# Final norm applied by tokens: TensorE turns the blocks of the finished sum, and one scaling by a column of roots per bank writes the output rows

## Chip, cores and metric

One core of a Trainium2 chip runs the whole program in one launch. The metric is device time in microseconds (us). The kernel before takes 1589.42 us, the median of three runs that lie between 1588.81 and 1590.37.

## The reference, cut to what matters

The program is a block of two layers (a gated MLP mixer with differential attention, then windowed attention with a sink; each followed by a SwiGLU) on 512 tokens of 1024 channels, with a context of 256 tokens beside them. What the change touches is the last line, the norm of the finished residual `h` (512 x 1024, float32) and its gain `g`:

```
def rmsnorm(x, g):
    xf = x.astype(jnp.float32)
    y = xf * lax.rsqrt(jnp.mean(xf * xf, axis=-1, keepdims=True) + EPS)
    return (y * g.astype(jnp.float32)).astype(x.dtype)
...
        h = h + g2 * swiglu(modulate(h, norm2_g[l], sh2, sc2), ffn_w_in[l], ffn_w_out[l])
...
    return rmsnorm(h, final_g)
```

## The kernel before, in words

Activations are kept transposed: channels on the 128 partitions, tokens along the free dimension. The residual is eight tiles `xT` of 128 channels x 512 tokens, held two by two, so that k = 0, 1 share a buffer (named 633 in the order of the program), 2 and 3 the next (634), 4 and 5 (635), 6 and 7 (636). Weights and activations are split in a high and a low part, and every product is three matmuls (`mm3`, L102 to L108).

The end of the program is the end of `ffn(1)`. The last product of the SwiGLU is summed in two halves of the tokens, first the tokens 256 to 511 (`off` = 256), then 0 to 255 (`off` = 0). For each half and each of the eight channel tiles m:

- `s2_part` runs the last matmuls on TensorE (PE) into a PSUM bank `pb` (L106 to L108), and `residual` (L774) adds the bank to `xT` on VectorE (DVE).
- `square` (L787) squares the finished piece on ScalarE (ACT). The squares of m = 0 to 4 are added up on GpSimd (POOL, L791) into `sq`; those of m = 5, 6 and 7 stay apart (`rest`).

Then the norm of a half: `rstd_diag` (L145) multiplies `sq` and the three other tiles with a block of ones, so that PE sums over the channels and a column per 128 tokens comes out (L156, L161). DVE takes the column, adds epsilon (L164), and makes the inverse root by a first guess and three Newton steps on 128 x 2 numbers (L135 to L139, ten instructions). Since tokens lie along the free dimension of `xT`, the roots must become rows: DVE writes them on the diagonals of a tile `dg` (L173), and PE multiplies it with ones (`spread`, L183), which gives a bank with the root of each token in all partitions. ACT copies that bank to `rs` for POOL (`final_rows`, L1484).

`final` (L1487) scales the eight tiles by gain and root. DVE does some in one instruction from the bank (L1496: k = 0 and 1 of the first half, k = 0 to 4 of the second), for the others ACT multiplies by the gain as soon as the squares are taken (L1493), and POOL by `rs` afterwards (L1494). After every second k, SyncE (SP) issues the store of 128 x 2 x 256 numbers (256 KB, in pieces of 1 KB, L1500) to `out`, which is 1024 x 512 and is turned on the host. There are eight such stores, four for each half.

The order on every engine is made by a scheduler from the order of the code, the pools' buffers and `issue_after`, which ties an instruction behind another.

Of the kernel before, what the change touches and what calls it, by code (L numbers as in the profile page):

```python
# [6 lines left out]
F32 = mybir.dt.float32  # L7
# [4 lines left out]
ALU = mybir.AluOpType  # L12
AX = mybir.AxisListType.X

P = 128
D = 1024
KT = D // P
TX = 512
# [8 lines left out]
class Builder:  # L27
# [69 lines left out]
    def dense(self, out, W, A, after=None, first=0):  # L97
        for k in range(len(W)):
            with self.tc.issue_after(after.ins) if after and k >= first else ExitStack():
                self.mm3(out, W[k], A[k], k == 0, k == len(W) - 1)  # L100

    def mm3(self, out, s, m, start, stop):  # L102

# [41 lines left out]
    def rstd_diag(self, accs, inv, bank=None, eps=None, at=None, more=()):  # L145

        nc = self.nc
        nb = sum(T for _, T in accs) // P
        ms = self.small(nb)
        o = 0  # L150
        for acc, T in accs:
            ps = (bank or self.bank)()
            n = T // P
            for j in range(n):
                c = slice(j * P, (j + 1) * P)
                self.last_sum = nc.tensor.matmul(ps[:, c], acc[:, c], self.ones, start=j == 0, stop=not more,  # L156
                                                 skip_group_check=True)
            for t in more:
                for j in range(n):
                    c = slice(j * P, (j + 1) * P)  # L160
                    nc.tensor.matmul(ps[:, c], t[:, c], self.ones, start=False, stop=t is more[-1], skip_group_check=True)  # L161
            col = ps[:, 0:T].rearrange("p (j f) -> p j f", f=P)[:, :, 0]
            if eps is None:
                nc.vector.tensor_scalar(ms[:, o:o + n], col, inv, EPS, ALU.mult, ALU.add)  # L164
            else:
                nc.vector.scalar_tensor_tensor(ms[:, o:o + n], col, inv, eps[:, o:o + n], ALU.mult, ALU.add)
            o += n
        r = self.rsqrt_small(ms, nb)
        dgs, o = [], 0
        for acc, T in accs:  # L170
            dg = at if at is not None else self.tmp()
            for j in range(T // P):
                self.last_diag = nc.vector.tensor_scalar(dg[:, j * P:(j + 1) * P], self.ident, r[:, o + j:o + j + 1], None,  # L173
                                                         ALU.mult)
            dgs.append(dg[:, :T])
            o += T // P
        return dgs
# [680 lines left out]
    def ffn(self, l):  # L858
# [190 lines left out]
        def s2_part(fs, m, W, off, n, chain=False):  # L1049
            ps = self.bank()[:, :n]  # L1050
            A = [(hi[:, off:off + n], lo[:, off:off + n]) for hi, lo in [hid[f] for f in fs]]
            if not chain:
                self.dense(ps, W, A)
                self.residual(l, 5, m, off, n, ps)
                return
            for k in range(len(W)):
                run("PE", self.mm3, ps, W[k], A[k], k == 0, k == len(W) - 1)
            run("DVE", self.residual, l, 5, m, off, n, ps)
# [418 lines left out]
        project(1, catB, lambda m: self.bank())  # L1477
        self.sq = sq, rest[1]

    def final_rows(self, sq, more, off, n):  # L1480
        dg = self.dg[:, off:off + n]
        r = self.rstd_rows(sq[:, off:off + n], n, 1.0 / D, self.single, dg, more, self.bank if off else self.fill)
        rs = self.p0.tile([P, 512], F32, name=self.uid("rs"), tag="tq"[off > 0], bufs=2)[:, :n]
        self.nc.scalar.copy(rs, r)  # L1484
        return r, rs

    def final(self, rows, off, n):  # L1487
        nc = self.nc
        r, rs = rows
        for k in range(KT):  # L1490
            g, h = self.gains[:, 4 * KT + k:4 * KT + k + 1], self.hx[k][:, off:off + n]
            if k >= (2, 5)[off == 0]:
                nc.scalar.mul(h, h, g)  # L1493
                nc.gpsimd.tensor_tensor(h, h, rs, ALU.mult)  # L1494
            else:
                nc.vector.scalar_tensor_tensor(h, h, g, r, ALU.mult, ALU.mult)  # L1496
            nh = self.nh
            if k % nh == nh - 1:
                out = self.a["out"][(k - nh + 1) * P:(k + 1) * P, off:off + n].rearrange("(k p) t -> p k t", p=P)
                nc.sync.dma_start(out, self.hxs[k // nh][:, :, off:off + n])  # L1500


def prep(inp):
# [15 lines left out]
    gains = np.concatenate([A["norm1_g"], A["norm2_g"], A["final_g"][None]], 0)  # L1519
    r["gains"] = c(gains.reshape(5 * KT, P).T)  # L1520
    ew = A["even_w_in"][0]
    r["qk"] = c(ew[:, 1024:2048].reshape(KT, P, 2, 2, 2 * P).transpose(3, 0, 1, 2, 4).reshape(2, KT, P, 512))
    r["v0"] = c(ew[:, 2048:2560])

# [49 lines left out]
```

## Time and profile before

| what | value |
|---|---|
| median of three runs | 1589.42 us |
| the profiled execution's own time | 1588.33 us |
| its span, first to last instruction | 1586.3 us |
| busy, PE / DVE / ACT / POOL | 96% / 68% / 46% / 52% |
| granted TensorE clock, mean | 0.988 |
| HBM written | 2.10 MB |
| end of the last residual product on PE | about 1570.2 us |
| last of the eight stores issued | 1582.63 us |

Times in the profile count from the start of the span. The profiled execution took 1588.33 us, of which 2.0 us lie around the span. PE is busy until 1570.2 us; what follows is the norm of the second half and the stores, 16 us in which PE works little.

### The profile page before, as it was taken

What the parts mean: (1) busy time and instruction counts of PE and PEld (TensorE: products, weight loads), DVE (VectorE), ACT (ScalarE), POOL (GpSimd) and SP (SyncE); (2) the same over time, 40 slices, a digit from 0 to 9 for tenths busy, and PEclk for the clock granted to TensorE, in tenths of its full rate; (3) what the DMA queues carried; (4) which work ended last, traced back from release to release, by engine and by line L of the source; (5) the groups of instructions that cost most, each with busy time, mean ns of one, the idle gap of its engine ahead of it and who ended that gap; (6) DMA issues with size and microseconds to landing.
All of it is one profiled execution on the core that took longest, in us unless ns stands there. A gap on an engine that the chain in (4) does not pass through costs nothing.

```text
span 1586.3 us, 24984 instructions
## 1 busy us (share of the span) xinstructions
PE 1518.7 (96%) x9547; PEld 1352.2 (85%) x9547; DVE 1084.7 (68%) x1958; ACT 723.3 (46%) x1472; POOL 830.7 (52%) x565
## 2 busy tenths in 40 slices
PE   6999988999999999999999989999999999999996
PEld 4776877889989999999999978777869989999996
DVE  4720788765688788888785585765667976666656
ACT  2412676553552333333333244565655644444443
POOL 0463211061256776677676415531304398888883
PEclk9999999999999999999999999999999999999998
DMA  8845100033223333454451012110225132323301
GB/s 328 308 145 188 40 8 1 3 131 133 67 80 113 114 120 106 140 166 147 164 165 57 27 52 80 61 34 14 68 80 206 54 120 88 113 92 109 94 14 54
DMA packets 54295, 162.00 MB, mean 102 GB/s; under 512 B 6176, under 2 KB 10656, under 8 KB 46496
## 3 DMA queue, kind: packets, MB, share of 16 engines
q1 hardware_dynamic: 47120, 135.11, 25.5%
q10 hardware_dynamic: 7056, 25.30, 4.9%
q8 instruction: 75, 1.23, 0.3%
q14 instruction: 44, 0.36, 0.1%
HBM read 158.29 MB, written 2.10 MB: 101 GB/s over the span
## 4 chain that ended last, share of the span: by engine, by line
PE 83%; DVE 10%; ACT 3%; issue 2%; DMA 1%; POOL 0%; POOLq 0%; SPq 0%; DVEq 0%; ACTq 0%
PE pw L106 11%; PE pw L107 11%; PE pw L108 11%; PE pb L107 8%; PE pb L106 8%; PE pb L108 8%; PE pf L106 4%; PE pf L107 4%; PE pf L108 4%; PE pb L1427 2%; PE pb L1416 2%; PE pf L359 2%; PE pw L1379 1%; PE pw L1387 1%; PE pw L542 1%
## 5 line engine op out<-in xcount | busy, mean ns | idle before, releaser
L84 POOL TENSOR_TENSOR w<-raw,w 128x512 fp32r<-128x512 f32 (+1 forms) x84 | 127.5, 1525 | 242.9 <-ACT w L81 220.5
L107 PE MATMUL pw<-ax,w 128*128 128x384 f32 (+2 forms) x732 | 233.9, 320 | 3.7 <-DVE ax L201 2.3
L106 PE MATMUL pw<-ax,w 128*128 128x384 f32 (+2 forms) x732 | 232.9, 322 | 4.1 <-DVE q L879 1.9
L108 PE MATMUL pw<-ax,w 128*128 128x384 f32 (+2 forms) x732 | 233.1, 320 | 0.1
L774 DVE SCALAR_TENSOR_TENSOR xT<-pb,mod,xT 128x512 f32<-128x512 f32 (+3 forms) x208 | 145.7, 707 | 125.8 <-PE pb L108 125.5
L879 POOL TENSOR_TENSOR w<-raw,w 128x512 fp32r<-128x512 f32 x110 | 169.4, 1555 | 19.7 <-ACT w L879 19.5
L879 POOL TENSOR_TENSOR w<-t,w 128x512 fp32r<-128x512 f32 x99 | 148.6, 1504 | 55.6 <-ACT w L879 55.6
L106 PE MATMUL pb<-hh,w 128*128 128x512 f32 x480 | 171.0, 356 | 2.3 <-DVE xT L774 2.3
L108 PE MATMUL pb<-hh,w 128*128 128x512 f32 x480 | 171.5, 357 | 0.3 <-DVE w L879 0.3
L107 PE MATMUL pb<-hh,w 128*128 128x512 f32 x480 | 171.1, 356 | 0.0
L107 PE MATMUL pw<-T,w 128*128 128x384 f32 (+1 forms) x508 | 156.9, 310 | 1.2 <-DVE T L123 1.2
L106 PE MATMUL pw<-T,w 128*128 128x384 f32 (+1 forms) x508 | 156.3, 310 | 1.1 <-DVE hs L879 1.1
L108 PE MATMUL pw<-T,w 128*128 128x384 f32 (+1 forms) x508 | 157.0, 310 | 0.0
L106 PEld LDWEIGHTS pw<-ax,w 128*128 128x128 f32 x732 | 138.5, 190 | 12.5 <-DVE q L879 2.6
L107 PEld LDWEIGHTS pw<-ax,w 128*128 128x128 f32 x732 | 139.0, 190 | 11.2 <-DVE ax L201 3.6
L106 PE MATMUL pf<-ax,w 128*128 128x256 f32 (+2 forms) x420 | 139.9, 333 | 7.9 <-DVE qf L252 5.0
L108 PEld LDWEIGHTS pw<-ax,w 128*128 128x128 f32 x732 | 139.2, 190 | 3.1 <-DVE w L948 0.4
L107 PE MATMUL pf<-ax,w 128*128 128x256 f32 (+2 forms) x420 | 138.8, 330 | 0.0
L108 PE MATMUL pf<-ax,w 128*128 128x256 f32 (+2 forms) x420 | 138.7, 330 | 0.0
L879 POOL TENSOR_TENSOR hh<-hs,hh 128x768 fp32r<-128x768 f32 (+1 forms) x42 | 80.7, 1922 | 90.0 <-ACT hh L879 67.6
L879 POOL TENSOR_TENSOR w<-rawo,w 128x512 fp32r<-128x512 f32 x59 | 103.5, 1754 | 30.1 <-ACT w L879 30.1
L228 DVE SCALAR_TENSOR_TENSOR junk<-ar,cb 128x1024 bf16<-128x1024 f32 x64 | 105.6, 1651 | 0.0
(378 smaller groups left out, 3936.8 us busy)
## 6 DMA issues: line engine op xcount, KB each, us to landing
raw<-ffn_in SPq DMA_DIRECT2D x44, 1024.0 KB, 5.1
ar<-ada SPq DMA_DIRECT2D x24, 1024.0 KB, 6.9
ar<-ada ACTq DMA_DIRECT2D x48, 512.0 KB, 3.5
rawo<-ffn_out SPq DMA_DIRECT2D x88, 256.0 KB, 3.0
raw<-odd_out SPq DMA_DIRECT2D x32, 256.0 KB, 2.7
raw<-qk SPq DMA_DIRECT2D x16, 256.0 KB, 7.9
raw<-uv SPq DMA_DIRECT2D x16, 256.0 KB, 2.7
raw<-even_out SPq DMA_DIRECT2D x8, 512.0 KB, 3.5
```

The lines of the kernel that those rows point to most:

```text
L84: eng.tensor_tensor(lo, raw, hi.bitcast(F32), ALU.subtract)
L106: mm(out, s[0], m[0], start=start, stop=False, **kw)
L107: mm(out, s[0], m[1], start=False, stop=False, **kw)
L108: return mm(out, s[1], m[0], start=False, stop=stop, **kw)
L228: return self.nc.vector.scalar_tensor_tensor(junk, t, 1.0, self.cb[who], ALU.mult, ALU.mult, accum_out=self.acc[who][:, col:col + 1])
L359: nc.tensor.matmul(ps[32 * q:32 * q + 32, :w], cst[:, k, :], t[:, w * q:w * q + w], start=k == 0, stop=k == KT - 1, skip_group_check=True)
L542: nc.tensor.matmul(ps[:, :TX], Q[c][:, qs], K[c][p][:, :TX], start=p == 0, stop=p == 1)
L774: ins = self.nc.vector.scalar_tensor_tensor(h, ps[:, r], self.modcol(l, j, m, who), h, ALU.mult, ALU.add)
L879: tail[key] = fn(*args, **kw)
L1379: nc.tensor.matmul(ps[:, st:en], Q, K[g][p][:, b0 * P:b1 * P], start=p == 0, stop=p == 1, skip_group_check=True)
L1416: last = nc.tensor.transpose(pt[:, x * P:(x + 1) * P], es[2 * (x % 2) + x // 2][:, kb * P:(kb + 1) * P], self.ident)
L1427: nc.tensor.matmul(po[64 * h:64 * h + 64, :], V[vb][:, 64 * g:64 * g + 64], t[:, h * TC:h * TC + TC], start=kb == 0, stop=kb == nb - 1, sk ...
```

## The change

The norm is applied with tokens on the partitions instead of channels.

- `rstd_diag` gets a way out that returns the column of roots `r` (128 tokens x 2) right after the Newton steps. The diagonals, the product with ones and the copy to `rs` are gone for the final norm, and with them `final_rows`.
- PE turns the finished `xT` in blocks of 128 x 128 (`transpose`), four blocks to a bank, so that a bank holds 128 tokens x 512 channels. There are 32 such transposes in eight banks. Those of a half's channels 512 to 1023 may start as soon as the last matmul of the second half's sum is issued (first half) or after the sum of squares (second half); the others are tied behind the sum of squares of the second half (`last_more`).
- A bank is written out with its root as a scalar per partition. The gain now lies along the free dimension: for the channels above `cut` x 128, DVE multiplies by the root and by a row of gains `gr` in one instruction (L1502); for the channels below, ACT has already multiplied `xT` by the gain in place (L1491, k = 0 to 5 in the first half and 0 to 3 in the second), and ACT multiplies by the root while it empties the bank (L1504). POOL has no part in it any more.
- The outputs go to four tiles `y` of 128 tokens x 1024 channels (16149 and 16150 of the first half, 16185 and 16186 of the second). Each is stored in two halves of 512 channels, eight stores of 256 KB in pieces of 2 KB (L1505), to `out`, which is now 512 x 1024. The host no longer turns it.
- One load is added, `gr`: the gains of the channels 512 to 1023, broadcast to all partitions (256 KB).

```
@@ rstd_diag
             for t in more:
                 for j in range(n):
                     c = slice(j * P, (j + 1) * P)
-                    nc.tensor.matmul(ps[:, c], t[:, c], self.ones, start=False, stop=t is more[-1], skip_group_check=True)
+                    self.last_more = nc.tensor.matmul(ps[:, c], t[:, c], self.ones, start=False, stop=t is more[-1],
+                                                      skip_group_check=True)
...
         r = self.rsqrt_small(ms, nb)
+        if at is False:
+            return r
@@ s2_part
-                self.dense(ps, W, A)
+                self.last_out = self.dense(ps, W, A)
@@ end of ffn
-            self.dg = Tp.tile([P, TX], F32, name="dg")
-            rows = [self.final_rows(sq, q, off, n) for q, (off, n) in zip(more, parts)]
-            for r, (off, n) in zip(rows, parts):
-                self.final(r, off, n)
+            gr = self.load(Tp, a["final"].partition_broadcast(P), [P, TX], "gr")
+            roots = [self.rstd_diag([(sq[:, off:off + n], n)], 1.0 / D, bank, None, False, q)
+                     for q, (off, n), bank in zip(more, parts, (self.single, self.fill))]
+            for r, (off, n), banks in zip(roots, parts, ([self.single] * 4, [self.single] + [self.bank] * 3)):
+                self.final(r, off, n, ring, banks, gr)
@@ final
-        r, rs = rows
-        for k in range(KT):
-            g, h = self.gains[:, 4 * KT + k:4 * KT + k + 1], self.hx[k][:, off:off + n]
-            if k >= (2, 5)[off == 0]:
-                nc.scalar.mul(h, h, g)
-                nc.gpsimd.tensor_tensor(h, h, rs, ALU.mult)
-            else:
-                nc.vector.scalar_tensor_tensor(h, h, g, r, ALU.mult, ALU.mult)
-            nh = self.nh
-            if k % nh == nh - 1:
-                out = self.a["out"][(k - nh + 1) * P:(k + 1) * P, off:off + n].rearrange("(k p) t -> p k t", p=P)
-                nc.sync.dma_start(out, self.hxs[k // nh][:, :, off:off + n])
+        H = D // 2
+        cut = (4, 6)[off > 0]
+        for k in range(cut):
+            h = self.hx[k][:, off:off + n]
+            nc.scalar.mul(h, h, self.gains[:, 4 * KT + k:4 * KT + k + 1])
+        rows = [pool.tile([P, D], F32, name=self.uid("y"), tag="w", bufs=12) for _ in range(n // P)]
+        for c in (H, 0):
+            for b in range(n // P):
+                ps, o = banks.pop(0)(), off + b * P
+                with tc.issue_after((self.last_out if off and c else self.last_more).ins):
+                    for j in range(0, H, P):
+                        nc.tensor.transpose(ps[:, j:j + P], self.hx[(c + j) // P][:, o:o + P], self.ident)
+                m = min(max(cut * P - c, 0), H)
+                s = r[:, b:b + 1]
+                if m < H:
+                    nc.vector.scalar_tensor_tensor(rows[b][:, c + m:c + H], ps[:, m:], s, gr[:, c + m - H:c], ALU.mult, ALU.mult)
+                if m:
+                    nc.scalar.mul(rows[b][:, c:c + m], ps[:, :m], s)
+                nc.sync.dma_start(self.a["out"][o:o + P, c:c + H], rows[b][:, c:c + H])
```

Up to the sums of squares of the first half, all engines keep their old order, but for the added load, which SP issues early in `ffn(1)` between two others. From there on ACT's multiplications by the gain stand one by one between its squares, and six rows of PE have changed places. After the last residual product PE's rows change most. Before, after the last residual product (bank pb_16086) come the sums of squares of the second half and the two spreads:

```order
L108 MATMUL pb_16086<-hh_15941,raw_15795 128x256
L156 MATMUL pw_16126<-ones,sq_15952 128x128 x2
L161 MATMUL pw_16126<-ones,sqs_16006 128x128 x2
L161 MATMUL pw_16126<-ones,sqs_16016 128x128 x2
L161 MATMUL pw_16126<-ones,sqs_16026 128x128 x2
L183 MATMUL pb_16121<-dg,ones 128x256
L183 MATMUL pf_16150<-dg,ones 128x256
```

In the changed kernel the eight transposes of the first half's upper channels stand ahead of those sums, and 24 more transposes behind them (the rows go on with three `pb` banks, and with pw_16187 as the last):

```order
L109 MATMUL pb_16086<-hh_15941,raw_15795 128x256
L1498 MATMUL pw_16151<-ident_100,xT_635_3304 128x128 x2
L1498 MATMUL pw_16151<-ident_100,xT_636_3306 128x128 x2
L1498 MATMUL pw_16159<-ident_100,xT_635_3304 128x128 x2
L1498 MATMUL pw_16159<-ident_100,xT_636_3306 128x128 x2
L157 MATMUL pf_16121<-ones,sq_15952 128x128 x2
L162 MATMUL pf_16121<-ones,sqs_16006 128x128 x2
L162 MATMUL pf_16121<-ones,sqs_16016 128x128 x2
L162 MATMUL pf_16121<-ones,sqs_16026 128x128 x2
L1498 MATMUL pw_16167<-ident_100,xT_633_3300 128x128 x2
L1498 MATMUL pw_16167<-ident_100,xT_634_3302 128x128 x2
```

So the spreads are gone, and the sums of squares start eight transposes later. On DVE the end of the first half's root (sm_16107), the diagonals and the root of the second half stood like this, with two scalings between the Newton steps:

```order
L139 SCALAR_TENSOR_TENSOR sm_16107<-sm_16108,sm_16107 128x2
L173 TENSOR_SCALAR dg<-ident_100,sm_16107 128x128 x2
L164 TENSOR_SCALAR sm_16125<-pw_16126 128x2
L135 TENSOR_SCALAR sm_16136<-sm_16125 128x2
L137 TENSOR_TENSOR sm_16137<-sm_16136 128x2
L138 SCALAR_TENSOR_TENSOR sm_16137<-sm_16137,sm_16125 128x2
L139 SCALAR_TENSOR_TENSOR sm_16136<-sm_16137,sm_16136 128x2
L137 TENSOR_TENSOR sm_16137<-sm_16136 128x2
L1496 SCALAR_TENSOR_TENSOR xT_633_3300<-xT_633_3300,gains_140,pb_16121 128x256 x2
L138 SCALAR_TENSOR_TENSOR sm_16137<-sm_16137,sm_16125 128x2
```

Now two pieces of the first half's output stand in the diagonals' place, and the last three Newton rows are followed by the two scalings that end the program on DVE (the rows left out between the two fences are the other Newton steps):

```order
L140 SCALAR_TENSOR_TENSOR sm_16108<-sm_16109,sm_16108 128x2
L1502 SCALAR_TENSOR_TENSOR y_16149<-pw_16151,sm_16108,gr_16095 128x256
L1502 SCALAR_TENSOR_TENSOR y_16150<-pw_16159,sm_16108,gr_16095 128x256
L166 TENSOR_SCALAR sm_16120<-pf_16121 128x2
L136 TENSOR_SCALAR sm_16131<-sm_16120 128x2
L138 TENSOR_TENSOR sm_16132<-sm_16131 128x2
```

```order
L138 TENSOR_TENSOR sm_16132<-sm_16131 128x2
L139 SCALAR_TENSOR_TENSOR sm_16132<-sm_16132,sm_16120 128x2
L140 SCALAR_TENSOR_TENSOR sm_16131<-sm_16132,sm_16131 128x2
L1502 SCALAR_TENSOR_TENSOR y_16185<-pw_16187,sm_16131,gr_16095 128x512
L1502 SCALAR_TENSOR_TENSOR y_16186<-pb_16194,sm_16131,gr_16095 128x512
```

The bank of the first of these two, pw_16187, is the one that PE fills last; pb_16194, which the second one reads, is filled three banks earlier.

More of the change, by code (lines that the diff above doesn't have):

```diff
@@ L99, in dense @@
             with self.tc.issue_after(after.ins) if after and k >= first else ExitStack():
-                self.mm3(out, W[k], A[k], k == 0, k == len(W) - 1)
+                ins = self.mm3(out, W[k], A[k], k == 0, k == len(W) - 1)
+        return ins
     def mm3(self, out, s, m, start, stop):
@@ L1478, in odd, with final @@
         self.sq = sq, rest[1]
[L1480 to L1488, printed above, removed]
-        r, rs = rows
-        for k in range(KT):
-            g, h = self.gains[:, 4 * KT + k:4 * KT + k + 1], self.hx[k][:, off:off + n]
-            if k >= (2, 5)[off == 0]:
-                nc.scalar.mul(h, h, g)
-                nc.gpsimd.tensor_tensor(h, h, rs, ALU.mult)
-            else:
-                nc.vector.scalar_tensor_tensor(h, h, g, r, ALU.mult, ALU.mult)
-            nh = self.nh
-            if k % nh == nh - 1:
-                out = self.a["out"][(k - nh + 1) * P:(k + 1) * P, off:off + n].rearrange("(k p) t -> p k t", p=P)
-                nc.sync.dma_start(out, self.hxs[k // nh][:, :, off:off + n])
+    def final(self, r, off, n, pool, banks, gr):
+        tc, nc = self.tc, self.nc
+        H = D // 2
[17 more added lines that the diff above has]
+                nc.sync.dma_start(self.a["out"][o:o + P, c:c + H], rows[b][:, c:c + H])
 def prep(inp):
@@ L1521, in prep @@
     ew = A["even_w_in"][0]
+    r["final"] = c(A["final_g"][D // 2:])
     r["qk"] = c(ew[:, 1024:2048].reshape(KT, P, 2, 2, 2 * P).transpose(3, 0, 1, 2, 4).reshape(2, KT, P, 512))
@@ L1568 @@
     a = {n: nc.dram_tensor(n, v.shape, mybir.dt.from_np(v.dtype), kind="ExternalInput").ap() for n, v in arrays.items()}
-    a["out"] = nc.dram_tensor("out", (D, TX), F32, kind="ExternalOutput").ap()
+    a["out"] = nc.dram_tensor("out", (TX, D), F32, kind="ExternalOutput").ap()
     with tile.TileContext(nc, schedule_with_timeline_sim=True) as tc:
@@ L1572 @@
     r = run_bass_kernel_spmd(nc, [arrays], core_ids=[0])
-    return np.ascontiguousarray(r.results[0]["out"].T)[None]
+    return np.ascontiguousarray(r.results[0]["out"])[None]
```

## Prediction

> **What bounds the kernel now.** The page and its chain of waits come first: the chain that ended last runs over PE for most of the program.
>
> ```profile
> span 1586.3 us, 24984 instructions
> PE 83%; DVE 10%; ACT 3%; issue 2%; DMA 1%; POOL 0%; POOLq 0%; SPq 0%; DVEq 0%; ACTq 0%
> ```
>
> The change leaves that part's order alone, so only the end can move. There I read PE's timeline for the end of its work.
>
> ```profile
> 1570.08 0.28 PE L108 MATMUL pb<-hh,raw 128*128 128x256 f32 x1
> 1570.20 0.61 PE L156 MATMUL pw<-ones,sq 128*128 128x128 f32 x4
> 1570.64 1.50 PE L161 MATMUL pw<-ones,sqs 128*128 128x128 f32 x12
> 1572.33 0.70 PE L183 MATMUL pb<-dg,ones 128*128 128x256 f32 x2 [0.19 <-DVE dg L173]
> 1578.23 1.22 PE L183 MATMUL pf<-dg,ones 128*128 128x256 f32 x2 [5.20 <-DVE dg L173]
> ```
>
> The last product starts at 1570.08. The sums of squares of the second half end at 1572.14, and then PE waits 5.20 us for the second half's diagonals. DVE's timeline tells why they are late.
>
> ```profile
> 1571.40 0.16 DVE L138 SCALAR_TENSOR_TENSOR sm<-sm,sm 128x2 f32<-128x2 f32 x1
> 1571.59 0.16 DVE L139 SCALAR_TENSOR_TENSOR sm<-sm,sm 128x2 f32<-128x2 f32 x1
> 1571.79 0.48 DVE L173 TENSOR_SCALAR dg<-ident,sm 128x128 f32<-128x128 f32 x2
> 1572.19 0.15 DVE L164 TENSOR_SCALAR sm<-pw 128x2 f32<-128x2 f32 x1
> 1573.47 0.87 DVE L1496 SCALAR_TENSOR_TENSOR xT<-xT,gains,pb 128x256 f32<-128x256 f32 x2
> 1574.26 0.68 DVE L138 SCALAR_TENSOR_TENSOR sm<-sm,sm 128x2 f32<-128x2 f32 x1
> 1577.01 0.65 DVE L139 SCALAR_TENSOR_TENSOR sm<-sm,sm 128x2 f32<-128x2 f32 x1
> 1577.69 0.48 DVE L173 TENSOR_SCALAR dg<-ident,sm 128x128 f32<-128x128 f32 x2
> 1579.95 2.05 DVE L1496 SCALAR_TENSOR_TENSOR xT<-xT,gains,pf 128x256 f32<-128x256 f32 x5 [1.77 <-ACT rs L1484]
> ```
>
> The same Newton instruction on 128 x 2 numbers takes 0.16 us at 1571.59 (one every 0.19) and 0.65 at 1577.01. What differs is POOL:
>
> ```profile
> 1573.51 4.13 POOL L1494 TENSOR_TENSOR xT<-xT,rs 128x256 f32<-128x256 f32 x6 [3.68 <-ACT rs L1484]
> 1579.99 2.09 POOL L1494 TENSOR_TENSOR xT<-xT,rs 128x256 f32<-128x256 f32 x3 [2.35 <-ACT rs L1484]
> ```
>
> Its multiplications run from 1573.51 to 1577.64, just while the Newton steps are slow. The second root is done at 1577.66. Diagonals, spread and copy take until 1579.95, and the scalings of the second half until 1582.1. What ends the program are the stores: their issues on SP, the time to landing, and the rate in stretches.
>
> ```profile
> 1580.85 2.24 SPq L1500 DMA_DIRECT2D out<-xT  x4
> L1500 SPq DMA_DIRECT2D out<-xT x8: 372/384/457, 1574.4 to 1582.6; - x8
> DMA to landing us min/median/max: 2.1/2.2/2.7
> 1579.60:1581.50 1.90, 0.00 (x0) 0.00 (x0) 1.55 (x4) 0.31 (x1) 1.51 (x3) 0.50 0.00 0
> 1581.50:1585.00 3.50, 0.00 (x0) 0.00 (x0) 0.49 (x2) 0.00 (x0) 0.58 (x1) 0.50 0.91 300
> 1585.00:1586.30 1.30, 0.00 (x0) 0.00 (x0) 0.00 (x0) 0.00 (x0) 0.00 (x0) 0.50 0.00 0
> GB/s 0 0 0 0 0 0 0 0 0 0 129 344 342 234 193 326 6 291 234 0 0 0 0 162 328 316 342 354 338 258 0 0 0 0 0 0 16 0 0 0
> ```
>
> The last four stores are issued from 1580.85 on, the last one at 1582.6. Nothing moves before 1581.5, and 1.05 MB then go at 300 GB/s until 1585.0 (the last row has slices of 0.5 us from 1570; full ones reach 340). 1.3 us later the span ends. So the end hangs on when the last stores are issued, and on their rate: 256 KB take 0.77 us at 340 GB/s, 0.87 at 300.
>
> **The change, step by step.** I lay the new rows on the old clock from 1570.20.
>
> *Transposes.* The nearest row is the same form in the attention, four 128 x 128 blocks against the identity:
>
> ```profile
> 1103.69 0.60 PE L1416 MATMUL pb<-ident,e 128*128 128x128 f32 x4
> L1416 PE MATMUL pb<-ident,e x4: 272/272/273, 1103.7 to 1104.0; 128*128 128x128 f32 x4
> ```
>
> One takes 0.272 us, four take 0.60, so one starts every (0.60 - 0.272) / 3 = 0.11 us: each transpose is one matmul, where a product of floats with ones is two (16 for eight rows above, 0.11 each too). Bounds: 0.09 (a fifth faster) to 0.272 (no overlap at all). I take 0.11, since it is the same instruction. Their inputs are ready: ACT multiplies the first half by the gains between its squares, at most 0.5 us each.
>
> ```profile
> L787 ACT ACTIVATE sqs<-xT 128x256 f32<-128x256 f32 x14 | 5.7, 411 | 2.3 <-DVE xT L774 2.3
> L1493 ACT ACTIVATE xT<-xT,gains 128x256 f32<-128x256 f32 x9 | 4.2, 497 | 0.1
> 1570.53 0.83 ACT L787 ACTIVATE sqs<-xT 128x256 f32<-128x256 f32 x2
> ```
>
> There are ten such multiplications now against nine, in a stretch where ACT had room; the last square still hangs on DVE's last residual and ends about 1571.4. A square that comes late behind a gain would hold PE's sums of the first half; I set nothing for it, at most 0.5 us.
>
> *Sums of squares.* Eight transposes stand ahead: 8 x 0.11 = 0.9. They end at 1573.0 instead of 1572.1, a loss of 0.9. The last square (1571.4) is needed at 1572.5, so it doesn't hold them.
>
> *Root of the second half.* DVE first does the two pieces of 128 x 256 from 1571.8 on, in the diagonals' place, at the 0.87 that the two scalings of that size took, done by 1572.7. Then come eleven small instructions at 0.195 = 2.15, for POOL is idle now: from 1573.05 to 1575.2. Before they took from 1572.19 to 1577.66, with the two scalings in between. So the root comes 2.4 us earlier. If they stayed slow for a reason other than POOL, the five that took 3.4 us from 1574.26 on would cost 2.4 more.
>
> *From root to output.* Diagonals, spread and copy (1577.69 to 1579.95, 2.26 us) are gone. PE's other 24 transposes go from 1573.0 to 1575.65, and the last bank is whole at 1575.8: this, not the root at 1575.2, is late next. Prices of emptying a bank of 128 x 512:
>
> ```profile
> L774 DVE SCALAR_TENSOR_TENSOR xT<-pb,mod,xT 128x512 f32<-128x512 f32 x2 | 1.5, 748 | 0.0
> L1419 ACT COPY pt<-pb 128x512 f32<-128x512 f32 x40 | 23.4, 585 | 23.0 <-PE pb L1416 22.9
> ```
>
> DVE's two (0.75, the second one 0.68 behind a neighbour) end at 1577.2; the first waits for the last bank, and the second, whose bank was full long before, stands behind it. ACT empties two banks of the first half until 1574.8, and from the root on the other two until 1576.5, at 0.6 each; if the column as a factor costs what L1493 takes over L787 (0.09), 0.2 later, and off the path.
>
> *Stores.* By these ends SP issues them at about 1572.35, 1572.75, 1574.25, 1574.8, 1576.0, 1576.6, 1577.25 and, one issue (0.46) later, 1577.7. SP issues in its code's order: the last store, whose ACT piece is done at 1576.5, stands behind the one that waits for DVE at 1577.2. The old last issue stood 2.4 us ahead of the last packet (1582.6 to 1585.0). So now 1577.7 + 2.4 = 1580.1. By the rate: six stores from 1575.15 (0.9 after the third's issue) at 0.77 to 0.87 us give 1579.8 to 1580.4. Both agree. That pieces are 2 KB and no longer 1 KB, I count as nothing; no store of that shape is in the trace.
>
> *The added load.* SP issues it between these:
>
> ```profile
> 1213.34 3.38 SPq L879 DMA_DIRECT2D rawo<-ffn_out  x6
> 1224.38 0.33 SPq L813 DMA_DIRECT2D raw<-ffn_in  x1
> 1259.76 1.66 ACT L879 CAST w<-raw 128x512 fp32r<-128x512 f32 x3
> ```
>
> SP had nothing to issue from 1216.7 to 1224.38, so an issue of 0.4 us fits; 256 KB more are 0.8 us for the load behind it. ACT's casts at 1259.76 still read the two tiles loaded before that one, so the delay has over 35 us to vanish in; without that cover it would cost 0.8.
>
> **Sum.** Last packet 1585.0 before, 1580.1 now: -4.9 us. In terms: sums +0.9; the root's own length -3.3 (5.47 to 2.15); diagonals to copy -2.3; from the copy, now from the root, to the last issue -0.2 (2.7 to 2.5). Span 1586.3 - 4.9 = 1581.4, time 1588.33 - 4.9 = 1583.4 for an execution like the profiled one. The median of the runs lies 1.1 above that one, so I say **1584.5**.
>
> **A rule against it.** The granted clock in stretches of one microsecond, before:
>
> ```profile
> 1573.20:1574.20 1.00, 0.00 (x0) 0.00 (x0) 0.85 (x3) 0.24 (x1) 0.69 (x2) 1.00 0.00 0
> 1574.20:1575.20 1.00, 0.00 (x0) 0.00 (x0) 0.97 (x3) 0.00 (x0) 1.00 (x3) 1.00 0.00 0
> 1575.20:1576.20 1.00, 0.00 (x0) 0.00 (x0) 0.97 (x2) 0.00 (x0) 1.00 (x2) 0.64 0.93 305
> ```
>
> After PE's matmul that ended at 1573.03 the clock stayed at 1.00 for 2.4 us, and then fell to 0.50. The Trainium skill, in "TensorE: Matmul & The Clock Gate", Part 4 (PE-mode transpose), says that transposes don't count as PE being busy, so that the full clock doesn't engage for them. The trace can't contradict it, as its transposes stand between other matmuls. By that rule the clock would fall 2.4 us after the sums (1573.0), at 1575.4, when two transposes are left: nothing lost. If it fell sooner, it is the first rival.
>
> **Rivals.**
> 1. *The clock falls at once behind the sums* (the rule at its worst). 24 transposes at 0.22 instead of 0.11: last bank 2.7 us later, last issue 1580.4, -2.2 in all: 1587.2, no change that can be told. For: the drop above. Against: it took 2.4 us. 0.08.
> 2. *Small waits add up* (a square behind a gain, hand-overs between PE, DVE and ACT, an ACT piece that is slow with a root per partition): 1.7 us or more lost of 4.9, near 1587. 0.09.
> 3. *Stores become the bound, slower than before.* The eight stores start to move at 1573.25 on one queue. At the old rate they need 7 us; if pieces of 2 KB at a pitch of 4 KB went at 0.45 of it (135 GB/s), 8 x 1.94 = 15.5: last packet 1588.8, span +3.8, time 1593.2. It decides at 8 x 1.47 us, 178 GB/s, where the last packet lands as before. For: the shape is new. Against: nothing in the trace shows longer pieces to be slower. 0.06, a third of it milder.
> 4. *Nothing is won*, since transposes don't overlap: at 0.272 the 32 take 8.7 us, PE ends at 1570.2 + 8.7 + 1.8 = 1580.7 and the last issue is 1582.7, as before: 1589.5. Against: the row of four in 0.60. 0.03.
>
> **Chances and range.** A measurement of this kernel can tell about 0.2% (3.2 us) from no change. The forecast, a gain of 3.2 to 6 us, has 0.74, and that is faster. Within 0.2%: rivals 1, 2, a third of 3, and most of 4, 0.21. Slower: the rest of 3 and of 4, 0.05. The range reaches from 1583.0 (transposes at 0.09 and stores at 340 GB/s, less a run's scatter of 0.8) to 1587.6 (rivals 1 and 2); left out are rivals 3 and 4 and a little below.
>
> **What would show it.** Right: no POOL row after the sums; Newton steps of the second half at 0.16 to 0.19; eight groups of four transposes in about 0.45 each; DVE's last instruction near 1577.2; the last store issued near 1577.7; the clock at 1.00 until about 1575.5. Wrong: transposes at 0.2 or more apart; Newton steps at 0.6 without POOL; stores in flight without a gap below 200 GB/s; or any shift ahead of 1560, which would speak for the added load.

## The result, and the profile after

The changed kernel takes 1583.8 us (median of 6 runs, 1583.37 to 1585.5), the kernel before 1590.2 on the same chip (6 runs, 1588.81 to 1592.09): a ratio of 0.9962 with a 95% interval of 0.9952 to 0.9973, some 6 us. Six more runs of the same file, told below, give a ratio of 0.9970 (0.9959 to 0.9981), some 4.9 us. The prediction was 1584.5. A ratio is formed over the undisturbed runs, here all of them, and need not equal the quotient of two medians.

The profiled execution takes 1584.4 us with a span of 1582.6. First PE's timeline from the last product on. Columns here and in all timelines: start, busy time, engine, line, operation, tiles, count, and in brackets the idle time ahead with what ended it.

```profile
1571.40 1.04 PE L1498 MATMUL pw<-ident,xT 128*128 128x128 f32 x8
1572.28 0.61 PE L157 MATMUL pf<-ones,sq 128*128 128x128 f32 x4
1572.72 1.50 PE L162 MATMUL pf<-ones,sqs 128*128 128x128 f32 x12
1574.06 1.04 PE L1498 MATMUL pw<-ident,xT 128*128 128x128 f32 x8
1574.94 1.47 PE L1498 MATMUL pb<-ident,xT 128*128 128x128 f32 x12
1576.25 0.60 PE L1498 MATMUL pw<-ident,xT 128*128 128x128 f32 x4
```

Eight transposes stand ahead of the sums, 0.88 us from the first of them to the first sum. The wait of 5.20 us for the diagonals is gone, and the last transpose ends at 1576.85. Next DVE's timeline of the same kernel, from the first half's two pieces on.

```profile
1573.06 0.88 DVE L1502 SCALAR_TENSOR_TENSOR y<-pw,sm,gr 128x256 f32<-128x256 f32 x2
1574.26 0.16 DVE L166 TENSOR_SCALAR sm<-pf 128x2 f32<-128x2 f32 x1 [0.33 <-PE pf L162]
...
1576.23 0.16 DVE L140 SCALAR_TENSOR_TENSOR sm<-sm,sm 128x2 f32<-128x2 f32 x1
1576.89 0.75 DVE L1502 SCALAR_TENSOR_TENSOR y<-pw,sm,gr 128x512 f32<-128x512 f32 x1 [0.50 <-PE pw L1498]
1577.56 0.74 DVE L1502 SCALAR_TENSOR_TENSOR y<-pb,sm,gr 128x512 f32<-128x512 f32 x1
```

The second root runs from 1574.26 to 1576.39 without a slow step: its first and last instructions, nine others between them, take 0.16 each. Behind it DVE waits 0.50 for the last bank and is done at 1578.30. ACT's timeline follows, and POOL's last row.

```profile
1573.58 0.86 ACT L1504 ACTIVATE y<-pw,sm 128x256 f32<-128x256 f32 x2 [1.03 <-DVE y L1502]
...
1576.48 1.26 ACT L1504 ACTIVATE y<-pb,sm 128x512 f32<-128x512 f32 x2 [0.52 <-PE pb L1498]
...
1569.38 1.58 POOL L795 TENSOR_TENSOR sq<-sq,sqs 128x256 f32<-128x256 f32 x2 [0.42 <-ACT sqs L791]
```

ACT's two pieces of the first half waited 1.03 for DVE; its last two end at 1577.74, ahead of DVE's. POOL has nothing to do after 1570.96. The stores: SP's issues, their time to landing, the rate in slices of 0.5 us from 1565, and stretches of the end (width, busy times of the engines, then the granted clock, the DMA share and GB/s).

```profile
L1505 SPq DMA_DIRECT2D out<-y x8: 332/336/407, 1574.1 to 1578.7; - x8
DMA to landing us min/median/max: 2.0/2.2/2.5
GB/s 0 0 0 0 0 0 0 0 0 0 0 33 0 0 0 0 0 0 0 41 389 385 385 385 385 127 348 389 365 393 377 225 0 0 0 16 0 0 0 0
1579.50:1580.00 0.50, 0.00 (x0) 0.00 (x0) 0.00 (x0) 0.00 (x0) 0.00 (x0) 1.00 1.03 393
1580.00:1580.50 0.50, 0.00 (x0) 0.00 (x0) 0.00 (x0) 0.00 (x0) 0.00 (x0) 0.60 0.99 377
1581.00:1582.60 1.60, 0.00 (x0) 0.00 (x0) 0.00 (x0) 0.00 (x0) 0.00 (x0) 0.50 0.00 0
```

The last store is issued at 1578.7, the bytes go at 365 to 393 GB/s where a slice is full, and the last packet is gone at 1580.8, in the slice that shows 225. There is one short gap, the slice of 127 from 1577.5. The clock is still at 1.00 at 1580.0, 3.1 us behind the last transpose.

**The tail.** Up to the last product only the added load, ACT's multiplications and six rows of PE differ, yet the last product ends 1.2 us later in this execution than in the one before. So I compare tails: from PE's first row behind the last product to the end of the span. Before it is 1570.20 to 1586.3, 16.1 us; now 1571.40 to 1582.6, 11.2. The difference of 4.9 is the predicted sum.

### The profile page after: what moved, and what is told of

It reads as the page before. It is cut to its first block, busy times and chain, and to the rows that moved or that the text cites. A ratio compares the mean times of both kernels' runs of the same rounds, so it can differ in the third digit from the quotient of the medians.

```text
span 1582.6 us, 25033 instructions
## 1 busy us (share of the span) xinstructions
PE 1520.8 (96%) x9575; PEld 1356.2 (86%) x9575; DVE 1080.4 (68%) x1951; ACT 725.9 (46%) x1477; POOL 825.5 (52%) x556
## 4 chain that ended last, share of the span: by engine, by line
PE 85%; DVE 9%; ACT 4%; issue 2%; DMA 0%; SPq 0%; POOL 0%; DVEq 0%; ACTq 0%; POOLq 0%
PE pw L107 11%; PE pw L108 11%; PE pw L109 11%; PE pb L108 8%; PE pb L109 8%; PE pb L107 8%; PE pf L107 4%; PE pf L108 4%; PE pf L109 4%; PE pb L1432 2%; PE pb L1421 2%; PE pf L363 2%; PE pw L1384 1%; PE pw L1392 1%; DVE t L883 1%
## 5 line engine op out<-in xcount | busy, mean ns | idle before, releaser
L883 POOL TENSOR_TENSOR w<-raw,w 128x512 fp32r<-128x512 f32 x110 | 169.0, 1551 | 19.7 <-ACT w L883 19.5
```

The source lines that it names most:

```text
L883: tail[key] = fn(*args, **kw)
```

## The experiments

The theory: the second root became shorter by 3.3, by 2.4 because POOL no longer multiplies beside it and by 0.9 because the two scalings no longer stand between its steps; the way from the root to the output became shorter because diagonals, spread and copy are gone (-2.3); the transposes ahead of the sums cost 0.9, and load and stores are nearly free. The rivals: the steps of the root were slow for a reason of their own; the gain lies in the longer pieces of the stores; or something ahead of the tail changed. The tails of all runs come first, by PE's rows and the span; "root" is the time from the end of the second half's sums to the end of its root. Times are medians; the old kernel beside them is that of the same chip.

| run | tail from, to | tail us | root us | time us | old kernel us | ratio, 95% |
|---|---|---|---|---|---|---|
| old kernel | 1570.20, 1586.3 | 16.1 | 5.5 | | | |
| changed | 1571.40, 1582.6 | 11.2 | 2.2 | 1583.8 | 1590.2 | 0.9962 (0.9952-0.9973) |
| e_same | 1573.55, 1584.7 | 11.15 | 2.2 | 1584.8 | 1589.7 | 0.9970 (0.9959-0.9981) |
| e_load | 1570.70, 1586.9 | 16.2 | 5.5 | 1589.5 | 1589.7 | 1.0000 (0.9991-1.0010) |
| e_nopool | 1570.88, 1584.6 | 13.7 | 3.05 | 1587.1 | 1588.9 | 0.9993 (0.9983-1.0002) |
| e_pool | 1570.47, 1583.3 | 12.8 | 3.85 | 1585.8 | 1588.9 | 0.9988 (0.9977-0.9999) |
| e_poolbig | 1572.40, 1585.7 | 13.3 | 4.3 | 1586.8 | 1588.9 | 0.9987 (0.9977-0.9996) |
| e_poolset | 1571.40, 1583.0 | 11.6 | 2.55 | 1584.8 | 1588.9 | 0.9968 (0.9957-0.9978) |
| e_first | 1571.06, 1584.3 | 13.2 | 2.2 | 1587.0 | 1589.3 | 0.9980 (0.9971-0.9989) |
| e_second | 1572.19, 1587.4 | 15.2 | 5.5 | 1588.7 | 1589.3 | 0.9990 (0.9981-0.9999) |
| e_second2 | 1569.57, 1583.3 | 13.7 | 5.55 | 1586.5 | 1589.7 | 0.9982 (0.9973-0.9992) |
| e_1kb | 1572.66, 1584.2 | 11.5 | 2.2 | 1585.7 | 1589.3 | 0.9976 (0.9966-0.9986) |
| e_order | 1572.26, 1583.4 | 11.1 | 2.2 | 1585.2 | 1589.3 | 0.9967 (0.9954-0.9979) |
| e_clock | 1571.06, 1590.6 | 19.5 | 2.2 | 1592.3 (one run) | 1589.7 | |

The starts of the tails lie between 1569.57 and 1573.55, and even the two profiled executions of the changed kernel are 2.15 apart there, while their tails agree within 0.05. Medians of a few runs can't settle a term of half a microsecond here; tails are the better measure, though every run has one trace alone and only the changed kernel has two.

### Is it POOL? (e_nopool, e_pool)

From the old kernel, the first half's multiplications on POOL are taken out:

```diff
-                nc.gpsimd.tensor_tensor(h, h, rs, ALU.mult)
+                if off == 0:
+                    nc.gpsimd.tensor_tensor(h, h, rs, ALU.mult)
```

> The old kernel without the six multiplications of the first half on POOL: those six blocks of the first half of the tokens are left without their root. Theory: the five slow Newton steps come down from 0.65 to 0.16 us, the second root ends at about 1575.2 in place of 1577.7, and the time falls by 2.4 us, to about 1587.7 where the old kernel gives 1590.2. Rival (slow for another reason): the steps stay at 0.65, and the time does not change.

DVE's timeline in that run:

```profile
1574.15 0.87 DVE L1497 SCALAR_TENSOR_TENSOR xT<-xT,gains,pb 128x256 f32<-128x256 f32 x2
1574.94 0.15 DVE L138 SCALAR_TENSOR_TENSOR sm<-sm,sm 128x2 f32<-128x2 f32 x1
...
1575.91 0.48 DVE L173 TENSOR_SCALAR dg<-ident,sm 128x128 f32<-128x128 f32 x2
```

The two scalings still stand in the middle of the root, but the steps behind them are at 0.15 to 0.16. The root takes 3.05 in place of 5.5 and the tail shrinks by 2.4, as expected. What is left above the changed kernel's 2.2 is the 0.87 of the two scalings. Three stores of the first half also leave earlier here, from 1563.89 on, but in the old kernel nothing was in flight when the second half's stores began, so that doesn't touch the end. The median fell by only 1.85 us, with an interval that just holds no change. Then the reverse: POOL's work is put into the changed kernel, hung on the first piece of output that DVE writes.

```diff
                 nc.sync.dma_start(self.a["out"][o:o + P, c:c + H], rows[b][:, c:c + H])
+                if off and c and not b:
+                    y = rows[b][:, c + m:c + H]
+                    for _ in range(6):
+                        nc.gpsimd.tensor_tensor(self.tmp()[:, :256], y, y, ALU.mult)
```

> The changed kernel, with six dummy multiplications of 128 x 256 on POOL (SBUF to SBUF, as the old kernel's were) while DVE works out the second root; their results are not used. Theory (the second root became short because POOL no longer multiplies beside it): the Newton steps of the second half take about 0.65 us each while POOL runs and 0.16 behind it, the root ends 2 to 3 us later, and so does the program: about +2.4 us against the changed kernel. Rival (the steps were slow in the old kernel for another reason, such as the two scalings between them or the state of DVE): the steps stay at 0.16 and the time does not change.

DVE's timeline of that run, and POOL's row:

```profile
1573.33 0.16 DVE L166 TENSOR_SCALAR sm<-pf 128x2 f32<-128x2 f32 x1 [0.34 <-PE pf L162]
1573.52 0.37 DVE L136 TENSOR_SCALAR sm<-sm 128x2 int32<-128x2 int32 x1
1573.92 0.53 DVE L138 TENSOR_TENSOR sm<-sm 128x2 f32<-128x2 f32 x1
1574.49 0.54 DVE L139 SCALAR_TENSOR_TENSOR sm<-sm,sm 128x2 f32<-128x2 f32 x1
...
1576.20 0.16 DVE L139 SCALAR_TENSOR_TENSOR sm<-sm,sm 128x2 f32<-128x2 f32 x1
...
1572.68 3.47 POOL L1509 TENSOR_TENSOR q<-y 128x256 f32<-128x256 f32 x6 [2.65 <-DVE y L1502]
```

POOL ends at 1576.15, and the step at 1576.20 is the first fast one again. The tail grows by 1.6. That is less than the 2.4 I expected: the dummies, which read one tile twice, took 3.47 us in place of 4.13 and began ahead of the root, so four steps were held in place of five, and for 0.53 in place of 0.65; the first estimate took 0.37 in place of 0.17. The cause is shown from both sides, and the rival is out.

### How does POOL hold DVE? (e_poolbig, e_poolset)

Six POOL instructions in 3.47 us, 0.58 each, and a step that takes 0.53 and starts 0.57 behind the last: one DVE step passes per POOL instruction. To tell a wait for the end of an instruction from an even sharing, three instructions of twice the size take the place of the six:

```diff
                     y = rows[b][:, c + m:c + H]
-                    for _ in range(6):
-                        nc.gpsimd.tensor_tensor(self.tmp()[:, :256], y, y, ALU.mult)
+                    y2 = rows[b][:, H:]
+                    for _ in range(3):
+                        nc.gpsimd.tensor_tensor(self.tmp(), y2, y2, ALU.mult)
```

> As the run with six, but POOL's work is three multiplications of 128 x 512, so its busy time is the same. Theory in its strict form (DVE's small instruction waits until the POOL instruction that is running has ended, one passing per POOL instruction): the steps beside POOL take about 1.3 us each, three of them, and the root ends about 0.6 us later than beside six small ones. Rival (DVE and POOL share the access evenly, each slowed by a factor): the steps keep 0.65 us, and the root ends as beside six.

DVE's timeline, and POOL's row:

```profile
1575.45 0.73 DVE L136 TENSOR_SCALAR sm<-sm 128x2 int32<-128x2 int32 x1
1576.22 0.96 DVE L138 TENSOR_TENSOR sm<-sm 128x2 f32<-128x2 f32 x1
1577.21 0.96 DVE L139 SCALAR_TENSOR_TENSOR sm<-sm,sm 128x2 f32<-128x2 f32 x1
1578.20 0.16 DVE L140 SCALAR_TENSOR_TENSOR sm<-sm,sm 128x2 f32<-128x2 f32 x1
...
1575.12 3.04 POOL L1510 TENSOR_TENSOR q<-y 128x512 f32<-128x512 f32 x3 [3.16 <-ACT y L1504]
```

POOL's instructions take 1.01 each now, and the two steps beside them 0.96; three of 1.3 were expected, by the old kernel's longer multiplications, but the first of the three places fell to the first estimate (0.73). The root ends 0.45 later than beside six small ones (4.3 against 3.85), against 0.6 expected. So a step lasts as long as the POOL instruction it meets, and no even sharing. In the last form POOL only writes:

```diff
-                    for _ in range(6):
-                        nc.gpsimd.tensor_tensor(self.tmp()[:, :256], y, y, ALU.mult)
+                    q = self.tmp()
+                    nc.gpsimd.tensor_tensor(q[:, :16], y[:, :16], y[:, :16], ALU.mult)
+                    for _ in range(8):
+                        nc.gpsimd.memset(q, 0.0)
```

> As the run with six, but behind one small multiplication POOL only writes: eight memsets of 128 x 512, which read nothing from SBUF. If POOL being busy is what counts, the steps take 0.5 us and more as beside the multiplications, and the time is 2 us longer than the changed kernel's. If POOL's reading counts, they stay at 0.16, and the time does not change.

Again DVE's timeline and POOL's row:

```profile
1574.46 0.57 DVE L136 TENSOR_SCALAR sm<-sm 128x2 int32<-128x2 int32 x1
1575.06 0.16 DVE L138 TENSOR_TENSOR sm<-sm 128x2 f32<-128x2 f32 x1
...
1573.89 4.62 POOL L1511 MEMSET q<- 128x512 f32 x8
```

POOL is busy until 1578.51, and the Newton steps, with two inputs from SBUF each, keep 0.16. Only the one instruction with a single input, the root's first estimate, takes 0.57, about one memset (0.58). The tail is 0.4 longer. So it is POOL's reading that holds the steps with two inputs. The Trainium skill says just this in "SBUF — State Buffer", sections "SBUF: two separate sides" and "Who interferes with whom": a VectorE instruction with two inputs in SBUF contends with a GpSimd instruction that reads SBUF, not with one that only writes, and the pair of ports is held for a whole instruction. These runs agree with both, with 0.53, 0.96 and 0.16 us for the same steps.

### Halves (e_first, e_second, e_second2)

In e_first only the half that is finished first goes the new way, in e_second only the other; the second output tensor and its rearrangement on the host are left out here.

```diff
 # e_first
-            roots = [...]
-            for ...: self.final(...)
+            r = self.rstd_diag([(sq[:, off:off + n], n)], 1.0 / D, self.single, None, False, more[0])
+            rows = self.final_rows(sq, more[1], o2, n2)
+            self.final(r, off, n, ring, [self.single] * 4, gr)
+            self.final_old(rows, o2, n2)
 # e_second
+            rows = self.final_rows(sq, more[0], off, n)
+            r = self.rstd_diag([(sq[:, o2:o2 + n2], n2)], 1.0 / D, self.single, None, False, more[1])
+            self.final_old(rows, off, n)
+            self.final(r, o2, n2, ring, [self.single] + [self.bank] * 3, gr)
```

> Only the half of the tokens that is finished first goes the new way; the second half goes the old way by rows, with its diagonals, the spread of the root, the copy and POOL's three multiplications. By the theory POOL has nothing to do while the second root is worked out, so its steps take 0.16 us: this takes the terms +0.9 (sums) and -3.3 (root) and leaves the rest as it was, -2.4 us against the old kernel. Rival (the gain is in the way from the root to the output, or in the longer pieces of the stores): less than 1 us of gain.

The tail is 13.2, 2.9 us shorter than before; 2.4 was expected. The extra half is seen in PE's row of the spread, which the second half still has here:

```profile
1576.62 0.70 PE L187 MATMUL pf<-dg,ones 128*128 128x256 f32 x2 [1.86 <-DVE dg L177]
```

It takes 0.70 us, where the same two matmuls took 1.22 at 1578.23 in the old kernel: there the clock had already fallen to 0.50, here the spread starts 1.86 us behind PE's other work, and the clock is still at 1.00.

> Only the second half of the tokens goes the new way; the first half goes the old way, with POOL's six multiplications beside the second root. By the theory the Newton steps keep their 0.65 us beside POOL and the root ends 5.5 us behind the sums as in the old kernel; then diagonals, spread and copy are gone, -2.2 to -3 us against the old kernel (stores of both kinds share one queue of issues). If the two halves' gains are independent, this and the run with the first half alone add up to the whole change, about -5.

This one missed: the tail is 15.2, only 0.9 shorter. SP's timeline shows why.

```profile
1576.56 0.97 SPq L1507 DMA_DIRECT2D outT<-xT  x2
1580.65 0.34 SPq L1529 DMA_DIRECT2D out<-y  x1
1581.09 0.39 SPq L1507 DMA_DIRECT2D outT<-xT  x1
1581.57 0.95 SPq L1529 DMA_DIRECT2D out<-y  x2
1582.62 0.53 SPq L1507 DMA_DIRECT2D outT<-xT  x1
1583.23 0.63 SPq L1529 DMA_DIRECT2D out<-y  x1
```

The scheduler put a store of the second half, which waits for the root, ahead of two stores of the first half on SP's queue, so six of the eight stores went out from 1580.65 on. That is the experiment's own order. With the first half's stores ahead:

```diff
-                nc.sync.dma_start(out, self.hxs[k // nh][:, :, off:off + n])
+                self.last_store = nc.sync.dma_start(out, self.hxs[k // nh][:, :, off:off + n])
...
-                nc.sync.dma_start(self.a["out"][o:o + P, c:c + H], rows[b][:, c:c + H])
+                with tc.issue_after(self.last_store.ins):
+                    nc.sync.dma_start(self.a["out"][o:o + P, c:c + H], rows[b][:, c:c + H])
```

> Again only the second half goes the new way, but SP now issues all four stores of the first half ahead of those of the second (in the run before, a store of the second half was put ahead of two of the first, and held them until 1580.65). Theory: the root still ends 5.5 us behind the sums beside POOL's six multiplications; DVE ends 1.5 us behind the root, and the last store is issued 0.5 us behind that: the tail is 13.8 us (16.1 in the old kernel, -2.3). If the way from the root to the output was not worth that, the tail stays above 14.8 (as the 15.2 of the run before).

DVE's timeline from the middle of the root:

```profile
1573.82 0.69 DVE L139 SCALAR_TENSOR_TENSOR sm<-sm,sm 128x2 f32<-128x2 f32 x1
...
1576.58 0.65 DVE L140 SCALAR_TENSOR_TENSOR sm<-sm,sm 128x2 f32<-128x2 f32 x1
1577.34 0.75 DVE L1526 SCALAR_TENSOR_TENSOR y<-pw,sm,gr 128x512 f32<-128x512 f32 x1
```

The steps stay slow beside POOL, the root ends 5.55 us behind the sums, and the tail is 13.7: 2.4 less, as expected. The halves' gains of 2.9 and 2.4 make 5.3, against 4.9 for the whole; the half microsecond of the clock stands in both, since either half's change takes the spread out of the slow clock.

### Stores (e_1kb, e_order)

```diff
 # e_1kb; the output has the shape (4, TX, 256)
-                nc.sync.dma_start(self.a["out"][o:o + P, c:c + H], rows[b][:, c:c + H])
+                dst = self.a["out"][:, o:o + P, :].rearrange("a p f -> p a f")[:, c // 256:c // 256 + 2]
+                nc.sync.dma_start(dst, rows[b][:, c:c + H].rearrange("p (a f) -> p a f", f=256))
```

> The changed kernel, with each store's rows cut into two pieces of 1 KB in an output that holds four slabs of 256 columns; the host lays the slabs side by side, nothing else differs. Theory (the time is won ahead of the stores): the rate falls from 385 to the old 330 to 350 GB/s and costs 0.3 to 0.5 us on the last four stores. Rival (longer pieces are a main part of the gain): 1.5 us and more.

The rates in slices of 0.5 us from 1570:

```profile
GB/s 0 0 0 33 0 0 0 0 0 0 0 0 160 340 328 342 358 338 303 344 330 346 350 336 313 6 0 0 0 16 0 0 0 0 0 0 0 0 0 0
```

Full slices hold 303 to 358 GB/s where the changed kernel's held 365 to 393, without any gap, and the tail is 0.3 longer. As the theory had it; the rival is out.

```diff
 # e_order
-... ([self.single] * 4, [self.single] + [self.bank] * 3)
+... ([self.single] * 4, [self.bank] * 3 + [self.single])
```

> The changed kernel with the four banks of the second half in another order: the two that DVE empties are filled first, so that its first scaling does not wait 0.50 us for the last bank but starts at the root. If the prediction is right that the last bank is what the end waits for, the tail from the first transpose to the end shrinks by 0.4 to 0.5 us. Rival: from the first store of the second half on the stores go at their full rate, so the tail is set by that store and by 1.05 MB at 385 GB/s (2.7 us), and changes by less than 0.15 us.

DVE's timeline, then the rates from 1570:

```profile
1577.08 0.16 DVE L140 SCALAR_TENSOR_TENSOR sm<-sm,sm 128x2 f32<-128x2 f32 x1
1577.36 1.41 DVE L1502 SCALAR_TENSOR_TENSOR y<-pb,sm,gr 128x512 f32<-128x512 f32 x2
```

```profile
GB/s 0 0 0 33 0 0 0 0 0 0 0 160 389 381 373 381 385 115 385 385 356 385 389 111 0 0 0 16 0 0 0 0 0 0 0 0 0 0 0 0
```

DVE no longer waits for the last bank, but the tail is 11.1 against 11.15 and 11.2. The gap between the halves (115 here, 127 there) is still there, and behind it the 1.05 MB go at their full rate. So the wait of 0.50 us costs at most 0.1. What didn't move is the second half's first store. It is that of ACT's first piece, shown here as SP's row in the changed kernel and as ACT's row in e_order:

```profile
1577.20 0.33 SPq L1505 DMA_DIRECT2D out<-y  x1
1577.34 0.69 ACT L1504 ACTIVATE y<-pb,sm 128x512 f32<-128x512 f32 x1 [0.52 <-PE pb L1498]
```

SP issues it at 1577.20 in the changed kernel and at 1578.05 in e_order, both times 0.81 us behind the end of the root and 5.8 behind the start of the tail. That agrees with the rival, by which this store and the rate set the end; no run moves this store alone, so it is not shown by itself.

### The rest of the 6 us (e_same, e_load)

e_same is the changed kernel unaltered. e_load is the old kernel with one line, and the array that it reads:

```diff
+            gr = self.load(Tp, a["final"].partition_broadcast(P), [P, TX], "gr")
             self.dg = Tp.tile([P, TX], F32, name="dg")
```

> The changed kernel once more, unaltered, to tell scatter from effect in the 6.0 us of the medians, of which the tail behind the last product explains 4.9. If the remaining 1.1 us is scatter of the executions, more runs give a difference of 4.5 to 5.5 us against the old kernel and again a tail of 11.2 us (+- 0.1) from the first transpose to the end. If something ahead of the tail became faster, the difference stays at 6.

> The old kernel with the added load alone: the 256 KB of gains are brought into SBUF between the same loads of weights, and nothing reads them. Theory: it hides wholly, 0 (+- 0.8 us) against the old kernel, and the tail from the sums to the end stays 16.1 us. Rival (the load delays the weights behind it, or sets them to a better time): a difference of 1 us or more, in one direction or the other.

More runs of the changed kernel are 4.9 us ahead of the old one, and the load alone changes nothing (ratio 1.0000, tail 16.2). The 6.0 of the first ratio fits 4.9 and scatter; the intervals of the two sets overlap over most of their length.

### The clock (e_clock)

```diff
-                    for j in range(0, H, P):
+                    for j in list(range(0, H, P)) * (24 if not off and not c and b else 1):
```

> The changed kernel with the four transposes of one bank of the second half done 24 times over into the same bank (92 more, the same result), so that PE does nothing but transposes for 10 us and more behind the last sum. If transposes count as work for the clock, it stays at 1.00 until about 3 us behind the last transpose, they start 0.11 us apart throughout, and the program becomes about 10 us longer. If they do not count, the clock falls 2.4 to 6 us behind the last sum, the transposes from there on start about 0.22 us apart, and the program becomes 14 us longer or more.

PE's row of the added transposes, and stretches with the granted clock in the third column from the end:

```profile
1576.35 10.21 PE L1498 MATMUL pb<-ident,xT 128*128 128x128 f32 x92
```

```profile
1580.00:1584.00 4.00, 4.00 (x40) 4.00 (x38) 0.00 (x0) 0.00 (x0) 0.00 (x0) 1.00 0.00 0
1584.00:1586.50 2.50, 2.50 (x24) 2.31 (x22) 0.00 (x0) 0.00 (x0) 0.00 (x0) 1.00 0.03 7
1588.00:1589.00 1.00, 0.00 (x0) 0.00 (x0) 0.00 (x0) 0.00 (x0) 0.00 (x0) 1.00 0.68 262
1589.50:1590.00 0.50, 0.00 (x0) 0.00 (x0) 0.00 (x0) 0.00 (x0) 0.00 (x0) 0.50 0.00 0
```

The last sum ended at 1573.88 and the last transpose at 1586.56. The clock is at 1.00 through all 92, which take 10.21 us, 0.11 each, and for 2.4 us and more behind them; at 1589.50 it is at 0.50. Transposes keep the clock up here like other matmuls; whether they alone can raise a clock that has fallen, no run shows. The rule of the Trainium skill that I weighed in the prediction ("TensorE: Matmul & The Clock Gate", Part 4) differs from this measurement, and the measurement decides. The tail grew by 8.3 and not by 10, which fits that seven of the eight stores were issued by 1577.98, and only one was left behind the repeated bank.

## Why the prediction was right, point by point

- **Sums +0.9**: 0.88. Transposes start 0.11 us apart, as the row from the attention had it.
- **Root -3.3**: it takes 2.17 us behind the sums in place of 5.5. The cause that the prediction read from two timelines side by side is shown by taking POOL's work out of the old kernel (-2.4, the share of the slow steps) and by putting it into the new one (+1.6). The other 0.9 has nothing to do with POOL: it is the two scalings, which stood between the steps and now have their place ahead of them, where DVE waits for the sums anyway.
- **Diagonals to copy -2.3**: gone as said. What the prediction didn't see is that 0.5 of it was the low clock, at which the spread ran (1.22 against 0.70 in e_first).
- **Root to last issue -0.2**: 2.36 us from 1576.39 to 1578.75, against 2.68 before, from the copy. The reason given was wrong, though. The prediction called the last bank "late next"; filling DVE's banks first (e_order) took that wait away and won at most 0.1. What is late next is, by all that e_order shows, the second half's first store, which hangs on the root and ACT's first piece (1577.20), and behind it the rate: 1.05 MB at 385 GB/s are 2.7 us.
- **Longer pieces, counted as nothing**: worth 0.3 (e_1kb). The time from the last issue to the last packet is 2.05 in place of 2.4. The way from the last packet to the end is 1.8 in place of 1.3 us, so the sum came out as said by two errors against each other: that part is luck. The closing takes 1.7 to 1.8 in every run in which both halves go the new way and 1.3 to 1.5 in the others; why is open.
- **Load 0**: shown by e_load. A shift ahead of 1560, which I had named as a sign against it, is in the profile (1.2 us), but starts of one and the same kernel scatter by more. A square behind a gain, at most 0.5: PE did not wait at its sums.
- **ACT's pieces of the first half**: expected right behind the first root, they waited 1.03 us for DVE's pieces of the same banks. It should cost nothing, since the queue of stores runs empty later anyway (the slice of 127). Whether the bank or the common tile of output rows binds the two was not tried.
- **Rivals**: the clock (1) did not fall before 1580.0; of the waits (2), the one that a run took away was worth at most 0.1; the stores (3) went at 365 to 393 GB/s, not at 135; the transposes (4) overlap.
- **The time**: the medians of the two sets, 1583.8 and 1584.8, lie around 1584.5. The correction behind it, "the median of the runs lies 1.1 above that one", is no rule, though: the changed kernel's two profiled executions (1584.4 and 1586.5) lie 0.6 and 1.8 above their medians. It only undid that the old kernel's profiled execution was a quick one.

## What to carry to other kernels

Look at what POOL does beside a chain of small DVE instructions: each one with two inputs in SBUF can wait for a whole POOL instruction that reads, so five steps of 0.16 us became 3.4 us in the old kernel; move POOL's work to another engine or another time, or cut it smaller. At the end of a program ask of a wait whether it delays the first store of the last stretch or leaves the queue empty; here a wait of 0.50 us that did neither was worth at most 0.1, and bytes over rate set the end. Judge a change of a fraction of a per cent by a tail from a common event in the trace, which agreed within 0.05 us where whole executions differed by 2.

## What the runs showed of the hardware that I had not expected

- The same instruction on 128 x 2 numbers takes 0.16, 0.53, 0.65 or 0.96 us, without POOL or beside POOL instructions of 0.58, 0.69 and 1.01 us that read. Beside memsets it takes 0.16, but the single-input first estimate 0.57.
- Stores whose rows are 2 KB long go at 365 to 393 GB/s in full slices of the changed kernel, in pieces of 1 KB (e_1kb) at 303 to 358.
- The clock fell to 0.50 between 2.0 us (e_order) and 4.6 us (e_load) behind the last matmul, be it a transpose or another; where it had fallen, a spread of two matmuls took 1.22 us in place of 0.70.
